# A two-layer hybrid attention trunk: all projections by rows, transposes for q, k and gates on VectorE and DMA, rotation by rows

## The chip, the cores and the metric

The kernel runs on one core of a Trainium2 chip. The metric is the device time of one execution in microseconds (us). Engines are named as the profile names them: PE is TensorE (PEld its loading of the stationary operand), DVE is VectorE, ACT is ScalarE, POOL is GpSimd, SP is SyncE, which here only issues DMAs.

## The reference

Two layers work on x of 256 rows and 2048 columns, all in float32. Each layer normalises x, multiplies it by one wide matrix, runs four groups of attention (4 heads of 128 each) on the result, gates them, and multiplies their concatenation by a second matrix into the residual sum. Cut to what matters:

```python
h = rms_norm(x, norm_g)
p = split_columns(h @ w_in)                    # w_in: 2048 x 7700
fox  = forgetting_attention(q, k, v, log_sigmoid(p["fox_f"] + fb)) * silu(p["fox_g"])
q1, q2, k1, k2 = rope(diff_q, diff_k)          # partial rotary, 16 of 64 columns
diff = (softmax(q1 k1^T) - lam * softmax(q2 k2^T)) v
diff = rms_norm(diff, diff_norm_g) * (1 - lambda_init) * silu(p["diff_g"])
moba = softmax(rope(mq) rope(mk)^T) mv * silu(p["moba_g"])   # one block of 256 keys: causal attention
gla  = rms_norm(gated_linear_attention(gq, gk, gv, log_a), gla_norm_g) * silu(p["gla_g"])
x = x + concat(fox, diff, moba, gla) @ w_out   # w_out: 2048 x 2048
```

After the second layer x is normalised once more and is the output.

## The kernel before

**Products.** Every float32 operand of a large product is split in two parts, hi and lo (both of the type fp32r, which TensorE multiplies in one pass), and a product is the sum of hi x hi, hi x lo and lo x hi. `hTp` holds both parts of the transposed normalised x, `mTh` and `mTl` those of the transposed attention outputs. The weights stream from DRAM: SP loads a step's block (`raw`, 4 buffers), ScalarE makes its hi half (`hi_of`), VectorE its lo half (`lo_of`), three steps ahead of the product (`parts_of`, `prepare`; 4 buffers for each half).

**Steps.** `_blocks` (L104) lists the blocks of columns of both matrices, `_steps` (L142) cuts each into steps: four K tiles of 128 rows for blocks of up to 264 columns, else two. Both kernels have 304 steps, 152 a layer. In a block of the kind "rows" the activations are stationary and the weights move (up to 512 columns; the result has the rows of x on its partitions). In a block of the kind "cols" the weights are stationary and the activations move, hi and lo side by side, so that the result has the features on its partitions, as q and k are needed in a score. A "cols" block of 512 is made in two halves of 256. In `multiply` (L1272) a step of rows has 12 matmuls of 512 columns, a step of columns 16 of 512 and 256. in layer 0 the steps of the first three blocks (the halves of a column block count as two) take turns by group of four K tiles, since x arrives in four chunks; in layer 1 they stand one block after the other.

**1/rms.** The norm's row factor is applied after the projection. For rows it is a per-partition scale (`rows_of`, L520). For columns `spread_rms` (L491) spreads it over the free axis by two products on TensorE into `rb`, and `summed` and `columns` (L509, L516) add the two halves of a result and multiply by `rb`.

**Order of the work.** `main` (L1364 on) walks over the steps: prepare the weights three steps ahead, multiply, then `tick` the task generators. Each task (an attention group, a chunk of the new x, a gate) goes on to its next `yield` once a step as long as VectorE's and ScalarE's budget of estimated time (`Costed`) allows. A block's result is handled by its function in `dones` once its step is through (`settle`). So a `yield` is the unit of distance between two pieces of work, and all that an engine issues stands in its queue in program order. Tiles between the stages come from pools of fixed size (`Slots`): s4 tiles of 1024 elements (named four, 8 of them), s2 of 512 (two, 6), gates (2), and two PSUM tiles `side` for all products outside the projections.

**Turning.** What must be transposed goes through VectorE and DRAM: `turned` (L296) transposes 32 x 32 blocks with a STREAM_TRANSPOSE; `moved` (L310) writes the tile to DRAM (L316), pauses twice, reads it back with the blocks in their places by four DMAs (L321), and pauses twice more before the reader may be issued. All of these DMAs stand on POOL. The softmax probabilities and the outputs of differential attention and GLA take this way, and so do chunks 0 to 2 of layer 1's x (`make_hT`, L455); chunk 3, the last, is transposed on TensorE (`turn_x`, L293 in the profile). `make_hT`'s squares for the row factor (`square_sum`) run on ScalarE.

**Between the layers.** The last block of layer 0 is w_out's chunk 3; `residual` (L1104) adds each chunk of its result to x on VectorE and starts `make_hT`. Layer 1's first block needs all four chunks of the new `hTp`, chunk 3 last.

**The attention groups.** `softmax` (L735) and `attend_columns` (L793) serve FoX and MoBA: q and k come transposed, the probabilities are turned, the second product has v stationary and the result transposed, as `mT` needs it. Differential attention (`diff`, L994) has the probabilities stationary; they are turned with the order "n" (the head innermost), so that its stationary operand `z1[:, :, 2 * h]` is read with a step of four (z0) or eight (z1) elements. `rotated` (L934) turns q and k by a table of cosines over columns, a shuffle on VectorE and a product on GpSimd (L951). GLA sums q times k over each head's columns by products with the constant `heads` (its diagonal, `dg`) and spreads the result over the identity on GpSimd. Gains of the two inner norms are multiplied on GpSimd, and so are the tables for FoX's forget gates (`fox_forget`).

## Time and profile before

| | |
|---|---|
| device time, median of 3 runs | 953.79 us (953.33 to 955.54) |
| the profiled execution: its time | 948.82 us |
| the profiled execution: span of the trace | 947.0 us |
| busy: TensorE, VectorE, ScalarE, GpSimd | 932.3, 633.5, 474.3, 119.5 us |
| DMA | 186.98 MB in 54693 packets, mean 197 GB/s |

The profile is that of one execution, so its times are compared with its own span. The busy share of an engine tells how much work it has, the chain of work that ended last tells whose work set the end, and the list of waits tells for whom an engine stood. The largest groups after TensorE's products are the weights' halves, here with columns for the line, the engine, the operation, out<-in and count, then busy us, mean ns, and idle time before with its releaser:

```profile
L187 DVE TENSOR_TENSOR lo<-raw,hi 128x1024 fp32r<-128x1024 f32 (+3 forms) x301 | 380.6, 1270 | 264.1 <-ACT hi L187 263.8
L187 ACT ACTIVATE hi<-raw 128x1024 fp32r<-128x1024 f32 (+3 forms) x301 | 317.2, 1059 | 398.3 <-PE mm L289 368.5
```

All VectorE and ScalarE calls that the planner costs are recorded at one line (L187, the wrapper's), so groups are told apart by their tiles.

### The profile page before, as it was taken

The page shows a single profiled execution, that of the slowest core. Times are in us where ns is not written, and L with a number is a line of the kernel's source. Part 1 is how long each engine was busy: PE and PEld are TensorE (multiplying, and loading weights), DVE is VectorE, ACT ScalarE, POOL GpSimd, SP SyncE. Part 2 cuts the span into 40 slices and gives each one's busy share as a digit, 9 for nine tenths or more (in the row PEclk, how much of TensorE's full clock was granted, in tenths as well). Part 3 has the DMA queues.
Part 4 walks back from the last instruction along what each step waited for, and adds up shares of the span by engine and source line. Part 5 has one row for each costly group of instructions (what it writes and reads, how often), then busy time and mean ns, then how long its engine had stood idle before and what let it go on. Part 6 is the DMA issues. An engine that isn't in the chain of part 4 may idle for free.

```text
span 947.0 us, 13818 instructions
## 1 busy us (share of the span) xinstructions
PE 932.3 (98%) x5334; PEld 817.7 (86%) x5334; DVE 633.5 (67%) x852; ACT 474.3 (50%) x644; POOL 119.5 (13%) x140
## 2 busy tenths in 40 slices
PE   9999999999999999999989999999999999999996
PEld 7989889888888988888788898898888898888886
DVE  7666777767668777566556668666675777865563
ACT  7665534554574346455446544455446634554451
POOL 0010201201112211011100102102011031130000
PEclk9999999999999999999989999999999999999999
DMA  8766564875568477677755544657555685677552
GB/s 309 231 204 206 175 199 149 234 220 186 178 191 255 135 224 224 205 223 222 225 158 166 170 154 144 196 186 227 196 178 178 203 235 180 194 239 236 192 178 90
DMA packets 54693, 186.98 MB, mean 197 GB/s; under 512 B 7489, under 2 KB 8033, under 8 KB 54626
## 3 DMA queue, kind: packets, MB, share of 16 engines
q1 hardware_dynamic: 46592, 165.24, 55.0%
q0 software_dynamic: 6256, 18.88, 7.0%
q10 hardware_dynamic: 1778, 1.97, 0.8%
q8 instruction: 42, 0.69, 0.3%
q14 instruction: 25, 0.20, 0.1%
HBM read 175.58 MB, written 10.49 MB: 196 GB/s over the span
## 4 chain that ended last, share of the span: by engine, by line
PE 95%; DMA 2%; DVE 1%; issue 1%; ACT 0%; POOL 0%; POOLq 0%; DVEq 0%; SPq 0%; ACTq 0%
PE mm L289 85%; PE side L289 9%; DVE lo L187 1%; DMA raw<-in_weights 1%; DMA four<-turn 1%; DMA four<-in_xt 0%; DVE xs L187 0%; DVE hTp L187 0%; ACT hTp L187 0%; PE side L293 0%; DVE four L187 0%; POOL four L321 0%; ACT hi L187 0%; POOLq L1407 0%; POOL rf L420 0%
## 5 line engine op out<-in xcount | busy, mean ns | idle before, releaser
L187 DVE TENSOR_TENSOR lo<-raw,hi 128x1024 fp32r<-128x1024 f32 (+3 forms) x301 | 380.6, 1270 | 264.1 <-ACT hi L187 263.8
L187 ACT ACTIVATE hi<-raw 128x1024 fp32r<-128x1024 f32 (+3 forms) x301 | 317.2, 1059 | 398.3 <-PE mm L289 368.5
L289 PE MATMUL mm<-hTp,hi 128*128 128x512 f32 x1120 | 281.9, 394 | 0.0
L289 PEld LDWEIGHTS mm<-hTp,hi 128*128 128x128 f32 x1120 | 201.5, 189 | 37.0 <-issue 0.3
L289 PE MATMUL mm<-hi,hTp 128*128 128x512 f32 (+2 forms) x1024 | 197.5, 340 | 0.0
L289 PEld LDWEIGHTS mm<-hi,hTp 128*128 128x128 f32 x1024 | 161.0, 190 | 21.2 <-issue 0.5
L289 PEld LDWEIGHTS mm<-hTp,lo 128*128 128x128 f32 x1120 | 152.8, 190 | 11.0
L289 PE MATMUL mm<-hTp,lo 128*128 128x256 f32 x1120 | 156.1, 282 | 0.0
L289 PE MATMUL mm<-lo,hTp 128*128 128x512 f32 (+2 forms) x512 | 105.3, 338 | 0.1
L289 PE MATMUL mm<-hi,mTh 128*128 128x512 f32 (+1 forms) x256 | 95.2, 377 | 0.0
L289 PE MATMUL mm<-hi,mTl 128*128 128x512 f32 (+1 forms) x256 | 95.0, 376 | 0.0
L289 PEld LDWEIGHTS mm<-lo,hTp 128*128 128x128 f32 x512 | 81.8, 189 | 10.3 <-DVE lo L187 0.3
L289 PE MATMUL mm<-lo,mTh 128*128 128x512 f32 (+1 forms) x256 | 64.4, 376 | 0.0
L289 PEld LDWEIGHTS mm<-hi,mTl 128*128 128x128 f32 x256 | 48.2, 188 | 9.0 <-DVE mTl L187 0.3
L289 PEld LDWEIGHTS mm<-hi,mTh 128*128 128x128 f32 x256 | 48.2, 188 | 8.6
L289 PEld LDWEIGHTS mm<-lo,mTh 128*128 128x128 f32 x256 | 46.2, 188 | 8.8
L289 PE MATMUL side<-four,four 128*128 128x128 f32 (+1 forms) x320 | 41.0, 289 | 0.0
L289 PEld LDWEIGHTS side<-four,four 128*128 128x128 f32 (+1 forms) x320 | 38.0, 205 | 1.9 <-issue 1.4
L951 POOL TENSOR_TENSOR four<-four,two 128x1024 f32<-128x1024 f32 x8 | 20.9, 2607 | 109.4 <-DVE four L187 54.1
L321 POOL DMA_DIRECT2D four<-turn x52 | 28.4, 553 | 34.6 <-DMA turn<-four 16.8
L187 ACT ACT_TABLE_LOAD x24 | 30.8, 1283 | 1.9 <-DVE an L187 1.5
L187 DVE TENSOR_TENSOR both<-mm,both 128x512 f32<-128x512 f32 x35 | 23.9, 682 | 0.0
(160 smaller groups left out, 635.3 us busy)
## 6 DMA issues: line engine op xcount, KB each, us to landing
raw<-in_weights SPq DMA_DIRECT2D x272, 512.0 KB, 4.0
raw<-in_weights SPq DMA_DIRECT2D x16, 516.0 KB, 3.6
raw<-in_weights SPq DMA_DIRECT2D x15, 528.0 KB, 4.6
turn<-four POOLq DMA_DIRECT2D x13, 512.0 KB, 3.4
four<-turn POOLq DMA_DIRECT2D x52, 128.0 KB, 5.8
xs<-in_x SPq DMA_DIRECT2D x4, 512.0 KB, 4.6
four<-in_xt SPq DMA_DIRECT2D x3, 512.0 KB, 6.7
turn<-two POOLq DMA_DIRECT2D x6, 256.0 KB, 4.1
```

Source lines behind the costliest of these rows:

```text
L187: return f(*args, **kw)
L289: t_.matmul(out, lhsT, rhs, start=start, stop=stop)
L321: g_.dma_start(t[c * 32:(c + 1) * 32].rearrange("p q a b -> p q (a b)"), z[:, c].rearrange("(q i) e -> i q e", q=4))
L951: g_.tensor_mul(sw, sw, over(f[:, 1], H))
```

## The change

- **Form.** All blocks are rows now; nine blocks of 512 per layer (GLA's q and k in one, FoX's, differential attention's and MoBA's q and k, FoX's and MoBA's gates) change from columns. `spread_rms`, `summed`, `columns`, `gate_columns` and the tables over columns go.
- **Turning.** `projected` scales such a block on ScalarE (the gates with the SiLU in the same instruction), rotates it by rows where asked (`rotated`, on VectorE, with tables for each row), and turns it with `turned`, so each goes through DRAM. q of all groups and GLA's q and k are then copied by ScalarE into a tile whose columns are in their natural order (`natural_of`); k stays in the order of the turning, and the scores read it as `kT[:, :, kt * H + h]`.
- **Pauses.** `moved` has a third pause between the reads and the reader.
- **Differential attention** turns its probabilities in the order "j" and copies them with `natural_of` before the second product. The outputs of differential attention and GLA are copied the same way, and the norms' gains become this copy's per-partition scale.
- **GpSimd's products.** The tables of FoX's gates and GLA's diagonal are made on ScalarE, head by head; GLA's diagonal sums are made on VectorE from the rows.
- **Order of blocks.** Differential attention's q and k come ahead of FoX's second v block, and its gate behind MoBA's k. In layer 1 the first and third block take turns; the third accumulates in a `side` tile, in layer 0 as well.
- **x.** Chunks 0 and 1 of layer 1's x: ScalarE copies the product to `xs`, and a DMA on POOL adds the input x to it in place (`accum_op`); SP no longer loads these chunks of x. s4 has 10 tiles in place of 8.

```diff
@@ _blocks, _steps
+        for i, (c0, n) in enumerate((
+            (COL["gla_a"], 264),
+            (COL["gla_q"], 512),
+            (COL["gla_g"] + 248, 264),
...
+            (COL["fox_q"], 512),
+            (COL["fox_k"], 512),
+            (COL["diff_q"], 512),
+            (COL["diff_k"], 512),
+            (COL["fox_v"], 258),
+            (COL["fox_g"], 512),
+            (COL["diff_v"], 512),
+            (COL["moba_q"], 512),
+            (COL["moba_k"], 512),
+            (COL["diff_g"], 512),
+            (COL["moba_g"], 512),
+            (COL["moba_v"], 512),
+        )):
+            out.append(block("w_in", l, c0, n, "rows", turn=l if i in ((0, 1, 2), (0, 2))[l] else None))
...
-            key = (j // 4, i) if i < 3 else (9, i)
+            key = (i, 0, 0) if turn is None else (first.setdefault(turn, i), j // 4, i)
@@ moved, behind the four reads
         yield
         yield
+        yield
@@ make_hT
+        if l == 1 and chunk < 2:
+            c = slice(chunk * 512, chunk * 512 + 512)
+            yield
+            g_.dma_start(xs[:, :, c], x[0, :, c].rearrange("(m p) c -> p m c", p=P), accum_op=OP.add)
+            for _ in range(4):
+                yield
@@ row_stats: spread_rms, over, summed, columns go
-        yield from spread_rms(l, r)
...
-        v_.tensor_mul(store[:, half * 2:half * 2 + 2], summed(ps), over(env["rb", l], 2))
...
+    def natural_of(t, slots, parts=((slice(None), 1.0),)):
+        z = yield from slots.take([P, t.shape[2], P])
+        for part, scale in parts:
+            a_.activation(z[:, part].rearrange("p n (q j) -> p n q j", q=4), t[:, :, part].rearrange("p q n j -> p n q j"),
+                          AF.Copy, scale=scale)
+        slots.put(t)
+        return z
+
+    def projected(name, pool=None, heads_first=False, func=AF.Copy, turn=None, natural=None):
+        def done(l, ps):
+            nat = s4.get([P, 8, P])
+            rows_of(l, ps, nat.rearrange("p (a m) d -> p m a d" if heads_first else "p (m a) d -> p m a d", m=2), func)
+            tasks.append(run(l, nat))
+            return nat
+
+        def run(l, nat):
+            yield
+            if turn is not None:
+                yield from rotated(nat, *turn)
+            t, = yield from turned([(nat, pool or s4, "j")], lambda: s4.put(nat))
+            if natural:
+                t = yield from natural_of(t, s4, natural)
+                yield
+            env[name, l] = t
+            ready.add((name, l))
+
+        return done
+
+    def rotated(nat, name, half, width):
...
+        v_.tensor_mul(u, z[..., :rot], cos)
+        v_.tensor_mul(w[..., :half], z[..., half:rot], sin[..., :half])
+        v_.tensor_mul(w[..., half:], z[..., :half], sin[..., half:])
+        v_.tensor_add(z[..., :rot], u, w)
+        s2.put(t)
@@ finish_rows
-        yield from split_group(l, gi, t, lambda: s4.put(t), lambda z: z.rearrange("p h (m q j) -> p q (h m) j", m=2, q=4))
+        z = yield from natural_of(t, s4, ((slice(None), gain[:, 0 if gi == 1 else 1, l:l + 1]),))
+        yield
+        yield from split_group(l, gi, z.rearrange("p (h m) t -> p h (m t)", m=2), lambda: s4.put(z))
@@ gla_qk, gla
+        v_.scalar_tensor_tensor(own, nat[:, 0:4], 0.125, nat[:, 4:8], op0=OP.mult, op1=OP.mult)
+        dgs = sm.tile([P, 8], F32, name="dgs", bufs=2)
+        v_.tensor_reduce(dgs, own.rearrange("p n (x d) -> p n x d", x=2), axis=AX.X, op=OP.add)
...
-                matmul(dg[:, c:c + 2], own[:, pair, m * P:(m + 1) * P], heads, True, True)
...
-        g_.tensor_mul(sT.rearrange("p m h t -> p (m h) t"), ident[:, None, :].to_broadcast([P, 8, P]),
-                      dgs[:, :, None].to_broadcast([P, 8, P]))
+        for m in range(2):
+            for h in range(H):
+                c = (h // 2 * 2 + m) * 2 + h % 2
+                a_.activation(sT[:, m, h], ident, AF.Copy, scale=env["gla_dgs", l][:, c:c + 1])
+            yield
@@ softmax
-                    matmul(dst[:, h], qT[:, h, m * P:(m + 1) * P], kT[:, h, kt * P:(kt + 1) * P],
+                    matmul(dst[:, h], qT[:, m * H + h], kT[:, :, kt * H + h],
@@ fox_forget
-                g_.tensor_mul(z[:, m], after[:, None, :].to_broadcast([P, H, P]), pf[:, m, :, None].to_broadcast([P, H, P]))
+                for h in range(H):
+                    a_.activation(z[:, m, h], after, AF.Copy, scale=pf[:, m, h:h + 1])
+                yield
@@ diff
-        t0, t1 = yield from turned_p(p0[:, 0], p1[0], "n", s4, p0)
+        t0, t1 = yield from turned_p(p0[:, 0], p1[0], "j", s4, p0)
+        z0 = yield from natural_of(t0, s2)
+        z1 = yield from natural_of(t1, s4)
+        yield
...
-            matmul(o[:, 1, h], z1[:, :, 2 * h], vn[:, 0, h * P:(h + 1) * P], True, False)
+            matmul(o[:, 1, h], z1[:, 2 * h], vn[:, 0, h * P:(h + 1) * P], True, False)
@@ residual
-            for m in range(2):
-                v_.tensor_add(xs[:, m, c], ps[m], xs[:, m, c])
+            if l == 0 and chunk < 2:
+                for m in range(2):
+                    a_.activation(xs[:, m, c], ps[m], AF.Copy)
+            else:
+                for m in range(2):
+                    v_.tensor_add(xs[:, m, c], ps[m], xs[:, m, c])
@@ dones
+            projected("fox_q", natural=whole),
+            projected("fox_k"),
+            projected("diff_q", turn=turn_d, natural=whole),
+            started(diff, projected("diff_k", turn=turn_d)),
+            fox_v,
+            projected("fox_g", sgs, True, AF.Silu),
+            rows_v("diff_v"),
+            projected("moba_q", turn=turn_m, natural=whole),
+            started(moba, projected("moba_k", turn=turn_m)),
+            diff_gate,
+            projected("moba_g", sgs, True, AF.Silu),
+            rows_v("moba_v"),
```

How this moves instructions is seen at three places. The rows below are the engine's instructions in program order: line, operation, out<-in with the elements of the output, and how many alike follow each other.

First TensorE between the layers: the last rows of w_out's chunk 3 (`mm<-lo,mTh`), then layer 1's first block (264 columns, `mm<-hi,hTp`), and among it the eight transposes of chunk 3 of the new x (`side<-ct,xs`). Before:

```order
L289 MATMUL mm<-lo,mTh 128x512 x4
L289 MATMUL mm<-hi,hTp 128x264 x16
L289 MATMUL mm<-lo,hTp 128x264 x8
L293 MATMUL side_4258<-ct,xs 128x128 x8
L289 MATMUL mm<-hi,hTp 128x264 x16
L289 MATMUL mm<-lo,hTp 128x264 x8
L289 MATMUL mm<-hi,hTp 128x264 x16
L289 MATMUL mm<-lo,hTp 128x264 x8
L289 MATMUL mm<-hi,hTp 128x264 x16
L289 MATMUL mm<-lo,hTp 128x264 x8
L289 MATMUL mm<-hTp,hi 128x512 x8
L289 MATMUL mm<-hTp,lo 128x256 x8
```

and now, where `side_4008` is the accumulator of the third block:

```order
L282 MATMUL mm<-lo,mTh 128x512 x4
L282 MATMUL mm<-hi,hTp 128x264 x16
L282 MATMUL mm<-lo,hTp 128x264 x8
L286 MATMUL side_3993<-ct,xs 128x128 x8
L282 MATMUL side_4008<-hi,hTp 128x264 x16
L282 MATMUL side_4008<-lo,hTp 128x264 x8
L282 MATMUL mm<-hi,hTp 128x264 x16
L282 MATMUL mm<-lo,hTp 128x264 x8
```

The first step still stands ahead of the transposes; behind them two steps now follow for each chunk of x, and the 512-column block of GLA's q and k, which came in two halves by columns, comes after both blocks and by rows.

Then ScalarE at the same place: the weights' hi halves (`hi<-raw`), the squares of a chunk (`parts<-xs`), and the hi part of the new x from a turned chunk (`hTp<-four`) or from TensorE's transposes (`hTp<-side`). Before:

```order
L187 ACTIVATE hTp<-four_3928,ngt 128x256 x4
L187 ACTIVATE hi<-raw 128x1024 x4
L187 ACTIVATE two_4117,parts<-xs 128x512
L187 ACTIVATE two_4119,parts<-xs 128x512
L187 ACTIVATE hi<-raw 128x1024 x2
L187 ACTIVATE hi<-raw 128x1056 x2
L187 ACTIVATE hTp<-four_4096,ngt 128x256 x4
L187 ACTIVATE hi<-raw 128x1056 x2
L187 ACTIVATE hi<-raw 128x1024
L187 ACTIVATE hTp<-side_4258,ngt 128x256 x4
```

and now:

```order
L181 ACTIVATE two_3774,parts<-xs 128x512
L181 ACTIVATE two_3776,parts<-xs 128x512
L181 ACTIVATE hi<-raw 128x1024 x3
L181 ACTIVATE two_3844,parts<-xs 128x512
L181 ACTIVATE two_3846,parts<-xs 128x512
L181 ACTIVATE hi<-raw 128x1024 x2
L181 ACTIVATE hTp<-four_3753,ngt 128x256 x4
L181 ACTIVATE hi<-raw 128x1056 x3
L181 ACTIVATE hTp<-four_3823,ngt 128x256 x4
L181 ACTIVATE hi<-raw 128x1056 x2
L181 ACTIVATE hTp<-side_3993,ngt 128x256 x4
```

Chunk 1 is `four_3928` before and `four_3753` now, chunk 2 `four_4096` and `four_3823`. Chunk 1's reader stood ahead of chunk 2's squares and eight halves ahead of chunk 2's reader; now it stands behind these squares and three halves ahead of chunk 2's reader. From the squares of chunk 2 to its reader there were four halves and are five, from that reader to chunk 3's (`hTp<-side`) there were three and are two.

Last GpSimd's queue in layer 0 around MoBA: writes to DRAM (`turn<-`), reads back (`<-turn`), and the products that went. The probabilities of MoBA are `two_3485` and `four_3487`, `four_2828` and `four_3051` the shuffled parts of its q and k, and `four_3128` the output of differential attention. Before:

```order
L951 TENSOR_TENSOR four_2828<-four_2828,two_2740 128x1024
L420 TENSOR_TENSOR rsh<-pw,halfpow 128x8
L316 DMA turn_3152<-four_3128 128x1024
L321 DMA four_3128<-turn_3152 32x4x256 x4
L951 TENSOR_TENSOR four_3051<-four_3051,two_2740 128x1024
L316 DMA turn_3507<-two_3485 128x512
L316 DMA turn_3509<-four_3487 128x1024
L321 DMA two_3485<-turn_3507 32x4x128 x4
L321 DMA four_3487<-turn_3509 32x4x256 x4
```

and now, from MoBA's k (`four_2781`) on, with the output of differential attention in `four_3044`, the gate in `gate_3151` and the probabilities in `two_3194` and `four_3196`:

```order
L309 DMA turn_2801<-four_2781 128x1024
L314 DMA four_2781<-turn_2801 32x4x256 x4
L412 TENSOR_TENSOR rsh<-pw,halfpow 128x8
L309 DMA turn_3069<-four_3044 128x1024
L314 DMA four_3044<-turn_3069 32x4x256 x4
L309 DMA turn_3172<-gate_3151 128x1024
L309 DMA turn_3217<-two_3194 128x512
L309 DMA turn_3219<-four_3196 128x1024
L314 DMA gate_3151<-turn_3172 32x4x256 x4
L314 DMA two_3194<-turn_3217 32x4x128 x4
L314 DMA four_3196<-turn_3219 32x4x256 x4
```

The two rotation products are gone; q (just ahead of these rows) and k go through DRAM, and the gate's write stands ahead of the probabilities' writes and its four reads ahead of their eight.

More of the change, by code (lines that the diff above doesn't have):

```diff
@@ new lines, in rotated @@
+    def rotated(nat, name, half, width):
+        z = nat.rearrange("p (m a) (s w) -> p m (a s) w", m=2, w=width)
+        rot = 2 * half
+        g = z.shape[2]
+        t = yield from s2.take([P, 2, 2, g, rot])
+        u, w = t[:, 0], t[:, 1]
+        cos, sin = (turns[name][:, :, i][:, :, None, :].to_broadcast([P, 2, g, rot]) for i in range(2))
+        v_.tensor_mul(u, z[..., :rot], cos)
[3 more added lines that the diff above has]
+        s2.put(t)
@@ L1172, in hybrid_trunk @@
     for z in _BLOCKS:
-        if z["half"] != 1:
-            l, f = next(dones)
-        own = {COL["diff_q"]: ("rope_d",), COL["moba_q"]: ("rope_m",)}.get(z["c0"] if z["w"] == "w_in" else None, ())
-        blocks.append({"kind": z["kind"], "lhs": hT if z["w"] == "w_in" else mT, "n": z["n"], "per": z["per"],
-                       "done": f and (partial(f, l) if z["half"] is None else partial(f, l, half=z["half"])), "keys": {("r", l), ("rb", l)} | {(k, l) for k in own},
-                       "need": "h" if z["w"] == "w_in" else "m", "l": l})
+        l, f = next(dones)
+        blocks.append({"kind": z["kind"], "lhs": hT if z["w"] == "w_in" else mT, "n": z["n"], "per": z["per"], "done": f and partial(f, l),
+                       "keys": {("r", l)}, "need": "h" if z["w"] == "w_in" else "m", "l": l,
+                       "side": z["turn"] is not None and z["c0"] == COL["gla_g"] + 248})
     plan = []
@@ L1251, in first_rms @@
         power(r, t, 2)
-        yield from spread_rms(0, r)
+        env["r", 0] = r
+        ready.add(("r", 0))
     def parts_of(s):
@@ L1275, in multiply @@
         if s["first"]:
-            b["ps"] = side.get([P, 1024]) if b is blocks[2] else mm.tile([P, 1024], F32, name="mm")
+            while b["side"] and not side.free:
+                tick(False)
+            b["ps"] = side.get([P, 1024]) if b["side"] else mm.tile([P, 1024], F32, name="mm")
         ps = b["ps"]
@@ L1333, in prepare @@
     def prepare(i):
[L1334 to L1335 removed]
+        if 0 < i < 16 and i % 4 == 0:
+            split_xt([i // 4 * 4 + k for k in range(4)])
         if i < len(plan):
```

287 lines of the change are left out of this document (68 added, 219 removed).

## The prediction

> **What bounds the kernel now.** I read the page's busy shares and its chain first, then who waited for whom on TensorE, then the timelines of the stretches that the change touches.
>
> ```profile
> PE 932.3 (98%) x5334; PEld 817.7 (86%) x5334; DVE 633.5 (67%) x852; ACT 474.3 (50%) x644; POOL 119.5 (13%) x140
> PE 95%; DMA 2%; DVE 1%; issue 1%; ACT 0%; POOL 0%; POOLq 0%; DVEq 0%; SPq 0%; ACTq 0%
> PE side L293 <- DVE xs L187: 4.8, 1, 4.8
> PE side L361 <- DVE four L356: 1.3, 1, 1.3
> PE side L289 <- DVE four L187: 0.7, 1, 0.7
> ```
>
> TensorE is busy for 98% and carries 95% of the chain; in the list of waits (the last three rows: us, times, longest) it stops for another engine three times in all. So an edit counts if it shortens TensorE's own stream, removes the 4.8 us wait, or makes a new one. Work moved among VectorE, ScalarE and GpSimd counts only through new waits.
>
> **Projections by rows.** TensorE's timeline, first columns (a step of four K tiles by 256 outputs), then rows (two K tiles by 512 outputs: as many products). Columns: start, length, operation.
>
> ```profile
> 167.26 2.00 PE L289 MATMUL mm<-hTp,hi 128*128 128x512 f32 x8
> 169.10 1.11 PE L289 MATMUL mm<-hTp,lo 128*128 128x256 f32 x8
> 170.05 2.00 PE L289 MATMUL mm<-hTp,hi 128*128 128x512 f32 x8
> ...
> 275.83 1.98 PE L289 MATMUL mm<-hi,hTp 128*128 128x512 f32 x8
> 277.65 1.07 PE L289 MATMUL mm<-lo,hTp 128*128 128x512 f32 x4
> 278.55 1.98 PE L289 MATMUL mm<-hi,hTp 128*128 128x512 f32 x8
> ```
>
> From start to start a columns step takes 170.05 - 167.26 = 2.79 us with 16 matmuls, a rows step 2.72 us with 12. Nine blocks of 512 per layer change form: 9 x 8 x 2 = 144 steps, 144 x 0.07 = **-10.1 us**. Per matmul, 512 columns take 1.82 / 8 = 0.228 us and 256 take 0.95 / 8 = 0.119, which is 5 ns over half; over nothing but the 576 dropped matmuls the saving would be worth 17 ns each. The Trainium skill ("TensorE: Matmul & The Clock Gate", section "Back-to-back issue gap") gives a gap of N/2.4 + 2.5 ns: by it the 576 matmuls save 1.4 us, an estimate from that page. The measured steps above differ from it, and I go by them; that it is right after all is a rival below.
>
> **Differential attention's second product.** It now reads copies made contiguous by ScalarE, where before its stationary operand was read with a step of four or eight elements. Before, and beside it the same number of matmuls in MoBA, whose moving operand comes in runs of 32:
>
> ```profile
> 306.39 2.02 PE L289 MATMUL side<-four,two 128*128 128x128 f32 x8
> 308.24 3.97 PE L289 MATMUL side<-four,four 128*128 128x128 f32 x16
> 311.97 2.07 PE L289 MATMUL mm<-hTp,hi 128*128 128x512 f32 x8
> ...
> 386.57 0.38 PE L289 MATMUL side<-two,four 128*128 128x128 f32 x2
> 388.80 0.61 PE L289 MATMUL side<-four,four 128*128 128x128 f32 x4
> 389.17 0.48 PE L289 MATMUL mm<-hi,mTh 128*128 128x512 f32 x1
> ```
>
> 24 matmuls take 311.97 - 306.39 = 5.58 us, MoBA's 24 take 389.17 - 386.57 = 2.60. The new stationary operand is contiguous as MoBA's is: 2 x 2.98 = **-6.0 us**. The scores of all three attentions now stream k in runs of 32, which by the MoBA rows costs nothing.
>
> **Side products dropped.** The spreading of 1/rms over columns and GLA's diagonal sums leave TensorE:
>
> ```profile
> 494.47 0.60 PE L289 MATMUL side<-ct,rstd 128*128 128x128 f32 x4
> 494.83 1.40 PE L289 MATMUL mm<-hTp,hi 128*128 128x512 f32 x5
> ...
> 68.84 0.95 PE L289 MATMUL side<-ct,two 128*128 128x2 f32 x8
> 69.64 1.19 PE L289 MATMUL mm<-hi,hTp 128*128 128x512 f32 x4
> ```
>
> 0.36 + 0.80 us a layer, **-2.3 us**.
>
> **The boundary of the layers.** The 4.8 us wait, by engine (in brackets: idle before, and what ended it), and two windows (length, PE busy, granted clock, DMA share and GB/s):
>
> ```profile
> 449.93 1.28 DVE L187 TENSOR_TENSOR xs<-mm,xs 128x512 f32<-128x512 f32 x2
> 452.26 2.15 DVE L187 STREAM_TRANSPOSE four<-xs 128x512 f32<-128x512 f32 x2
> 454.71 0.56 POOL L316 DMA_DIRECT2D turn<-four  x1 [16.80 <-DVE four L187]
> 461.90 2.19 POOL L321 DMA_DIRECT2D four<-turn  x4 [6.63 <-issue]
> 469.12 2.87 ACT L187 ACTIVATE hTp<-four,ngt 128x256 fp32r<-128x256 f32 x4 [5.97 <-DMA four<-turn]
> 473.00 2.43 DVE L187 TENSOR_TENSOR lo<-raw,hi 128x1056 fp32r<-128x1056 f32 x2 [0.30 <-ACT hi L187]
> 475.35 1.28 DVE L187 TENSOR_TENSOR xs<-mm,xs 128x512 f32<-128x512 f32 x2
> 470.16 1.13 PE L289 MATMUL mm<-lo,hTp 128*128 128x264 f32 x8
> 476.09 2.35 PE L293 MATMUL side<-ct,xs 128*128 128x128 f32 x8 [4.80 <-DVE xs L187]
> 470.90:476.10 5.20, 0.40 (x5) 0.96 0.17 36
> 476.10:483.20 7.10, 6.98 (x34) 0.55 0.62 195
> ```
>
> Chunk 2 of the new x is turned through DRAM: transposed by 454.4, landed at 469.1. ScalarE stood in its queue for 5.97 us; behind it stood the weights' halves, behind those VectorE's sum of chunk 3, and behind that TensorE's transposes. TensorE stood 5.0 us and then ran at a clock of 0.55: the transposes take 478.09 - 476.09 = 2.0 us and the next 16 matmuls 3.66 (481.75 - 478.09, below) where the same 16 before took 1.95 (470.16 - 468.21).
>
> ```profile
> 468.21 2.11 PE L289 MATMUL mm<-hi,hTp 128*128 128x264 f32 x16
> 478.09 3.87 PE L289 MATMUL mm<-hi,hTp 128*128 128x264 f32 x16
> 481.75 0.64 PE L289 MATMUL mm<-lo,hTp 128*128 128x264 f32 x2
> ```
>
> With about 1.1 us too much in the transposes, 1.7 here and 0.4 in the rest of that step, the place costs 5.0 + 3.2 = 8.2 us. The interleaving of layer 1's blocks doubles the work ahead of chunk 3, but the transposes still stand after the first step, so by itself it is worth nothing here. What helps is the third pause in the turning: the reader stands six steps behind, not five (+2.7 us), with one conversion of weights less between it and the sum (-1.2). VectorE is also spared what delayed the sum at 449.93 (chunk 1's reader, which moves behind it), some 1.8 us. Landing at 467.3 plus 5.9 us of that chain is 473.2, against 471.1 for the end of TensorE's step: 2.1 us of standing. Against it, chunk 1's transfers now come just ahead on GpSimd's queue, for they wait for the new accumulating DMA of x; I add 1.1 us. TensorE stands 3.2 us at its own clock: **-5.0 us**. Bounds: landing as before leaves 3.9 us and the slow clock (-1.1); landing ahead of the reader leaves 0.6 (-7.6).
>
> **New transfers and who waits.** Nine more tiles a layer go through DRAM: 18 x 5 = 90 more DMAs on GpSimd, and 18 x 1.05 MB = 19 MB more.
>
> ```profile
> DMA packets 54693, 186.98 MB, mean 197 GB/s; under 512 B 7489, under 2 KB 8033, under 8 KB 54626
> 433.00:438.00 5.00, 5.00 (x24) 4.14 (x23) 2.45 (x2) 1.73 (x3) 2.19 (x4) 1.00 1.00 315
> L321 POOL DMA_DIRECT2D four<-turn x52 | 28.4, 553 | 34.6 <-DMA turn<-four 16.8 <-issue 16.8 <-DMA two<-in_const 1.1
> four<-turn POOLq DMA_DIRECT2D x52, 128.0 KB, 5.8
> 378.14 2.18 POOL L321 DMA_DIRECT2D four<-turn  x4 [0.24 <-issue]
> ```
>
> The mean rises to about 206 / 0.927 = 222 GB/s, under the 315 that a full window moved. An issue costs GpSimd 0.55 us (90 x 0.55 = 50 us, for the 50 us of products that leave it). A DMA on GpSimd is issued behind those before it, and each of the readers stands three pauses after its issue; ScalarE's copies that wait there have the hi halves of later weights behind them. Those run three steps ahead (8.2 us), less 2.3 for the two halves: some 6 us of a reader's waiting are free, and the longest wait of a reader above is 5.97, with the reader one step nearer. The Trainium skill ("SBUF — State Buffer", section "Who interferes with whom") says that GpSimd cannot write descriptors while VectorE holds their shared port: it speaks against 90 more such DMAs. In the trace an issue takes 553 ns in the mean with VectorE busy for 67%, so the sum stays; if VectorE's transposes or products held it, each would add its own 1.4 us, still within those 6.
>
> Tightest is MoBA's second product: its last read is issued at 379.8 and lands some 5.8 us later, 385.6, against 386.57 when TensorE takes it: 1.0 us of room. It moves one step earlier (+2.7), but behind four reads of the gate (-2.2) and in a stretch where 3.1 MB of turning meet 4.2 MB of weights in eight steps, 334 GB/s, over the 315. I take 1 us of waiting a layer, **+2.0 us** (bounds 0 and 6).
>
> ScalarE gains some 36 us (copies, per-head products, block evacuations) and VectorE loses about 45 (sums, 1/rms products, shuffles, against nine transposes a layer); at 54% and 62% both are covered by TensorE. The accumulating DMA has no row: between the 3.4 us of a 512 KB write and four times that, 14 us, it ends before its reader, about 15 us later; cost 0. The start and the end (8 us after the last matmul) stay.
>
> **Sum.** -10.1 - 6.0 - 2.3 - 5.0 + 2.0 = -21.4 us on the profiled execution's 948.8 (span 947.0 and 1.8 around it): 927.4. The median of the three runs shown lies 5.0 us higher, at 953.8, and the prediction is for such runs: 953.8 - 21.4 = **932.4 us**.
>
> **Rivals.**
> - *The waits eat a part.* The boundary keeps its stop (-1.1), MoBA waits 3 us a layer (+6): 953.8 - 10.1 - 6.0 - 2.3 - 1.1 + 6 = 940.3. For it: DMA shares of 1.00 around the boundary. Against it: readers a step later.
> - *A matmul costs its columns alone*, so the change of form brings only 1.4 us: 953.8 - (21.4 - 8.7) = 941.1. This is the page's rule above; against it stand 2.79 and 2.72.
> - *Slower: ScalarE's copies wait in its queue.* Seven such copies a layer read turned data. A single turn took 14.7 us at its slowest above and the reader comes some 13.8 us after the transpose; from about 20 us a turn, the weights' halves behind it come late and TensorE stands for the excess. At 23 us, 14 copies x 3 = 42 us: 953.8 - 23.4 + 42 = 972. It decides from 1.7 us a copy (23.4 / 14). For it: transfers overlap in threes (gate, two probabilities). Against it: no such length in this trace, and room in the DMA's mean.
> - *No change* takes the same waits at 1.7 us a copy, 14 x 1.7 = 23.8 against the gains of 23.4: 954.
>
> **Chances.** Forecast 0.74, waits 0.11, columns alone 0.03, slower 0.09, no change 0.03. The forecast's own range is 926 (-26.0, with the boundary at -7.6 and MoBA free, and 2 us for smaller gaps) to 937; up to 943 it takes in the first two rivals. A measurement of this kernel tells 0.2% (1.9 us) from no change. Faster 0.88, same 0.03, slower 0.09.
>
> **What would show it.** TensorE with some 4,730 matmul records instead of 5334 and rows steps of 2.72 us throughout; differential attention's 24 in 2.6 us; no granted clock of 0.55 at the boundary and under 4 us of standing there; MoBA's wait under 2 us. It is wrong if TensorE's list of waits shows hi or lo of weights, or ScalarE's copies waiting over 6 us for a turned tile.

## The result, and the profile after

| | before | changed |
|---|---|---|
| device time, median of 4 runs each | 953.56 us (951.24 to 955.54) | 939.65 us (939.12 to 944.78) |
| ratio to before, 95% interval | | 0.9867 (0.9826 to 0.9908) |
| the profiled execution: time, span | 948.82, 947.0 us | 939.94, 938.1 us |

The change made the kernel faster by 13.9 us by the medians, where 21.4 were forecast. The time lies 7 us above the point and outside the forecast's own range of 926 to 937; it is inside the wider range, up to 943, that takes in the first two rivals. Between the two profiled executions the gain is 8.9 us, because the one of before was faster than all the runs of before that were timed beside it, and that of the changed kernel lies at its median. Medians and ratios here leave out one slow run of one kernel (best2), which took over 1.5% more than that kernel's fastest.

The page of the changed kernel, busy times, DMA and the chain, then TensorE's list of waits (engine, what it waited for: us in all, times, longest):

```profile
PE 917.3 (98%) x4734; PEld 780.8 (83%) x4734; DVE 577.6 (62%) x782; ACT 505.5 (54%) x712; POOL 120.5 (13%) x204
DMA packets 60271, 204.56 MB, mean 218 GB/s; under 512 B 8977, under 2 KB 9265, under 8 KB 60210
PE 88%; DMA 5%; issue 3%; POOL 1%; DVE 1%; ACT 1%; POOLq 0%; DVEq 0%; ACTq 0%
```

```profile
PE side L282 <- DMA four<-turn: 7.8, 2, 4.1
PE side L286 <- DVE an L181: 1.5, 2, 0.8
PE side L286 <- DVE xs L181: 1.4, 2, 1.1
PE side L354 <- DVE four L349: 1.3, 1, 1.3
PE side L282 <- DVE eight L181: 0.3, 1, 0.3
```

600 matmul records fewer are the 576 of the form and the 24 of the dropped side products. TensorE's own stream is shorter, but its share of the chain fell from 95% to 88%: three waits are new or have moved. The 4.8 us for the sum of chunk 3 (`DVE xs`) became 1.4, MoBA's second product now waits twice 4 us for its turned probabilities, and the transposes of `an` in GLA's first block wait twice for VectorE. GpSimd is as busy as before: its products went and 88 DMAs came (90 for the turning and two that add x, less four small loads of constants).

TensorE's timeline of differential attention's second product, after; columns: start, length, operation:

```profile
285.97 1.05 PE L282 MATMUL side<-four,two 128*128 128x128 f32 x8
286.86 1.95 PE L282 MATMUL side<-four,four 128*128 128x128 f32 x16
288.57 1.17 PE L282 MATMUL mm<-hi,hTp 128*128 128x512 f32 x4
```

From 285.97 to 288.57 are 2.60 us, as forecast. At the boundary (the same view; in brackets the idle time before and what ended it) the stop is 1.1 + 0.3 us, with the granted clock at 1.00:

```profile
467.47 1.13 PE L282 MATMUL mm<-lo,hTp 128*128 128x264 f32 x8
469.73 0.33 PE L286 MATMUL side<-ct,xs 128*128 128x128 f32 x1 [1.12 <-DVE xs L181]
470.32 0.98 PE L286 MATMUL side<-ct,xs 128*128 128x128 f32 x7 [0.26 <-DVE xs L181]
471.06 2.18 PE L282 MATMUL side<-hi,hTp 128*128 128x264 f32 x16
```

The 16 matmuls behind the transposes take 2.0 us, not 3.66. What was lost stands at MoBA. GpSimd's queue in layer 0, TensorE beside it, and three windows (length, busy time of PE, PEld, DVE, ACT and POOL, granted clock, DMA share, GB/s):

```profile
359.04 0.56 POOL L309 DMA_DIRECT2D turn<-gate  x1 [11.22 <-DVE gate L181]
362.45 0.56 POOL L309 DMA_DIRECT2D turn<-two  x1 [2.85 <-DVE two L181]
363.57 0.54 POOL L309 DMA_DIRECT2D turn<-four  x1 [0.56 <-DVE four L181]
364.28 2.20 POOL L314 DMA_DIRECT2D gate<-turn  x4 [0.17 <-issue]
366.94 1.63 POOL L314 DMA_DIRECT2D two<-turn  x3 [0.46 <-issue]
369.73 0.55 POOL L314 DMA_DIRECT2D two<-turn  x1 [1.16 <-DMA turn<-four]
371.65 1.21 POOL L314 DMA_DIRECT2D four<-turn  x2 [1.36 <-DMA gate<-turn]
374.40 1.21 POOL L314 DMA_DIRECT2D four<-turn  x2 [1.54 <-DMA gate<-turn]
```

```profile
378.43 0.38 PE L282 MATMUL side<-two,four 128*128 128x128 f32 x2
382.54 1.19 PE L282 MATMUL side<-four,four 128*128 128x128 f32 x4 [3.72 <-DMA four<-turn]
```

```profile
370.20:378.40 8.20, 8.20 (x38) 6.79 (x37) 2.45 (x2) 4.22 (x5) 2.28 (x5) 1.00 1.03 282
378.40:382.60 4.20, 0.48 (x4) 0.28 (x2) 2.12 (x2) 1.17 (x2) 0.00 (x0) 0.96 1.02 297
382.60:386.50 3.90, 3.90 (x23) 3.90 (x23) 0.33 (x1) 0.00 (x0) 0.00 (x0) 0.60 0.76 287
```

The eight reads of the probabilities took from 366.94 to 375.61, 8.7 us. Before they took 4.6 (375.69 to 380.32); the first four of them, in the kernel before:

```profile
375.69 2.21 POOL L321 DMA_DIRECT2D two<-turn  x4 [3.58 <-DMA turn<-two]
```

The last read, issued at 375.06, landed 7.35 us later, at 382.4. TensorE was through with the two matmuls that do not need it at 378.8 and stood until 382.54. Behind the stop it ran at a clock of 0.60. The DMA share is 1.0 in the windows before and during the stop. Layer 1 is the same, with 4.1 us of standing and seven us at a clock of 0.51:

```profile
843.00:850.00 7.00, 6.22 (x26) 5.96 (x27) 2.38 (x2) 1.06 (x1) 0.00 (x0) 0.51 0.99 391
```

In this execution the clock was at half for 3.4 us behind the first stop and for 6.8 us behind the second, so 1.7 and 3.4 us were lost there. With the 7.8 us of standing, the two places cost 12.9 us.

### The profile page after: what moved, and what is told of

It reads as the page before. It is cut to its first block, busy times and chain, and to the rows that moved or that the text cites. A ratio compares the mean times of both kernels' runs of the same rounds, so it can differ in the third digit from the quotient of the medians.

```text
span 938.1 us, 12710 instructions
## 1 busy us (share of the span) xinstructions
PE 917.3 (98%) x4734; PEld 780.8 (83%) x4734; DVE 577.6 (62%) x782; ACT 505.5 (54%) x712; POOL 120.5 (13%) x204
## 4 chain that ended last, share of the span: by engine, by line
PE 88%; DMA 5%; issue 3%; POOL 1%; DVE 1%; ACT 1%; POOLq 0%; DVEq 0%; ACTq 0%
PE mm L282 78%; PE side L282 10%; DMA four<-turn 2%; DMA gate<-turn 2%; DMA turn<-four 1%; POOL four L314 1%; PE side L354 0%; DVE lo L181 0%; ACT hi L181 0%; DVE xs L181 0%; POOL gate L314 0%; ACT L181 0%; DVE four L181 0%; ACT hTp L181 0%; PE side L286 0%
## 5 line engine op out<-in xcount | busy, mean ns | idle before, releaser
L181 ACT ACTIVATE hi<-raw 128x1024 fp32r<-128x1024 f32 (+3 forms) x301 | 317.3, 1059 | 378.8 <-PE mm L282 318.4
L282 PE MATMUL mm<-hi,hTp 128*128 128x512 f32 (+2 forms) x2048 | 465.8, 371 | 0.0
L282 PEld LDWEIGHTS mm<-hi,hTp 128*128 128x128 f32 x2048 | 358.7, 188 | 66.3 <-issue 1.1
L282 PE MATMUL mm<-lo,hTp 128*128 128x512 f32 (+2 forms) x1024 | 249.8, 369 | 0.0
L282 PEld LDWEIGHTS mm<-lo,hTp 128*128 128x128 f32 x1024 | 181.0, 188 | 32.7
L314 POOL DMA_DIRECT2D four<-turn x108 | 59.2, 554 | 76.7 <-DMA turn<-four 38.6
L309 POOL DMA_DIRECT2D turn<-four x27 | 15.4, 569 | 348.0 <-DVE four L181 337.9
L282 PEld LDWEIGHTS side<-four,four 128*128 128x128 f32 (+1 forms) x320 | 37.1, 202 | 10.4 <-issue 9.5
L181 ACT ACTIVATE four<-mm,rstd 128x512 f32<-128x512 f32 (+2 forms) x56 | 33.6, 647 | 3.6 <-DVE fx L181 3.6
L181 DVE STREAM_TRANSPOSE four<-four 128x1024 f32<-128x1024 f32 x24 | 29.6, 1232 | 0.3
L181 ACT ACTIVATE four<-side,nb 128x256 f32<-128x256 f32 (+1 forms) x48 | 20.5, 436 | 2.0 <-DVE nb L181 1.9
L181 DVE COPY_PREDICATED four<-masks,side 128x128 f32<-128x128 uint8 x56 | 19.1, 341 | 1.8
```

The costliest lines, as they stand in the source:

```text
L181: return f(*args, **kw)
L282: t_.matmul(out, lhsT, rhs, start=start, stop=stop)
L309: g_.dma_start(via[-1], t.rearrange("p c a b -> p c (a b)"))
L314: g_.dma_start(t[c * 32:(c + 1) * 32].rearrange("p q a b -> p q (a b)"), z[:, c].rearrange("(q i) e -> i q e", q=4))
```

## The experiments

Each is an edit of the changed kernel, run beside the kernel before on the same chip; times are medians. Not all were run on one chip, so differences between them are also given by their ratios to before. The theory at their start: the forecast's terms hold but for MoBA's wait, which is larger; the rival: the terms themselves (form, boundary) were overrated.

### The form of the projections

```diff
+                if b["cols"]:                       # the nine blocks
+                    for c in range(4):
+                        wc, o = w[:, c * P:(c + 1) * P], ps[:, c % 2 * 512:c % 2 * 512 + 512]
+                        if part == "hi":
+                            matmul(o, wc, hTp[:, kt].rearrange("p z t -> p (z t)"), first and c < 2, False)
+                        else:
+                            matmul(o[:, :SEQ], wc, lh[:, kt], False, last and c > 1)
+                    continue
```

> The changed kernel with the product of the nine blocks a layer in the form by columns again (16 matmuls a step of 512 and 256 columns in place of 12 of 512), written into the same accumulators so that everything behind it runs as in the changed kernel; two of four chunks of outputs fall on each other, so the projections' values are left wrong. The forecast's term: 144 steps of 2.79 in place of 2.72 us, 10.1 us slower, 949 to 950. Theory of cost by columns alone: 1.4 us slower, 941. In the trace the steps of columns should show 2.79 us from start to start.

Measured 949.84 us (ratio to before 0.9962, 0.9944 to 0.9979): 10.2 us above the changed kernel's median, 9.1 by the ratios, whose intervals leave some 4 us on each side. Its TensorE timeline, two steps by columns:

```profile
300.49 2.00 PE L282 MATMUL mm<-hTp,hi 128*128 128x512 f32 x8
302.33 1.12 PE L282 MATMUL mm<-hTp,lo 128*128 128x256 f32 x8
303.29 2.00 PE L282 MATMUL mm<-hTp,hi 128*128 128x512 f32 x8
```

2.80 us from step to step, as before. The form is worth what the steps' difference says, and the cost by columns alone, 1.4 us, is refuted.

### MoBA's wait

Three kernels: the room for GpSimd's descriptors doubled (`dynamic_dma_scratch_size` 4096 to 8192, `T4` 10 to 9), the gate's turn two pauses later, and the gate's turn left out (the gate is then applied in a wrong order). In the second the wait for the gate also moves behind MoBA's second product, which reads only the probabilities and v. Its edit:

```diff
             if turn is not None:
                 yield from rotated(nat, *turn)
+            for _ in range(2 if name == "moba_g" else 0):
+                yield
@@ attend_columns
-        yield from until((name + "_g", l))
+        if name == "fox":
+            yield from until((name + "_g", l))
...
+        yield from until((name + "_g", l))
+        sgT = env[name + "_g", l]
         mixed = yield from s4.take([P, H, SEQ])
```

> The changed kernel with room for twice as many descriptors of GpSimd's DMAs (8192 bytes in place of 4096; one tile less in the pool of 1024-element tiles makes the place, and the order of all instructions stays). In the changed kernel GpSimd stood 1.36 and 1.54 us ahead of the last four reads of MoBA's probabilities in layer 0, put down to the gate's reads. Theory A, the descriptors' room limits how many DMAs GpSimd has under way: these stands go, the last read lands about 3 us earlier, TensorE's wait at MoBA's second product falls from 4 to 1 us a layer and with it the slow clock behind it; 930 to 934 us. Theory B, the transfers themselves are at the limit (windows there show a DMA share of 1.0): the reads are issued earlier and land as late as now; TensorE's wait stays at 3.5 to 4.3 us a layer, the time within 0.2% of the changed kernel's 939.7.

> The changed kernel with MoBA's gate turned two pauses later, so that its write stands behind the writes of MoBA's probabilities and its four reads behind their eight, and with the wait for the gate moved behind MoBA's second product. The bytes are the same. Theory A, the wait at MoBA's second product comes from the gate's DMAs standing ahead of the probabilities' on GpSimd's queue and rings: the wait falls below 1 us a layer, and the time to 927 to 932 us. Theory B, the DMA engines are full with weights and turns, whatever their order: the wait falls by half at most, 935 us or more. A third way: the gate now comes late, and TensorE stands at group 2 of the output projection instead, 938 us or more.

> The changed kernel without the turning of MoBA's gate (VectorE copies the tile where it transposed it, and its one write and four reads through DRAM are left out), so MoBA's gate is applied in a wrong order. Both theories of a cause in the gate's transfers (queue or bandwidth) expect the wait at MoBA's second product to be gone: under 0.5 us a layer, 926 to 931 us. If instead the cause is the transfers of the weights or the probabilities' own turn, the wait stays above 2 us a layer and the time above 934.

Measured: ring 941.84 us (0.9872, 0.9843 to 0.9901), gate_later 930.31 (0.9761, 0.9734 to 0.9787), gate_unturned 929.26 (0.9741, 0.9714 to 0.9769). GpSimd's queue in ring and in gate_later:

```profile
364.00 2.20 POOL L314 DMA_DIRECT2D gate<-turn  x4
366.43 2.17 POOL L314 DMA_DIRECT2D two<-turn  x4 [0.23 <-issue]
370.92 0.55 POOL L314 DMA_DIRECT2D four<-turn  x1 [2.31 <-DMA gate<-turn]
373.26 0.55 POOL L314 DMA_DIRECT2D four<-turn  x1 [1.79 <-DMA gate<-turn]
```

```profile
362.05 0.57 POOL L309 DMA_DIRECT2D turn<-two  x1 [13.77 <-DVE two L181]
362.61 0.56 POOL L309 DMA_DIRECT2D turn<-four  x1
363.71 0.54 POOL L309 DMA_DIRECT2D turn<-gate  x1 [0.54 <-DVE gate L181]
366.73 2.21 POOL L314 DMA_DIRECT2D two<-turn  x4 [2.48 <-DMA turn<-two]
368.93 2.20 POOL L314 DMA_DIRECT2D four<-turn  x4
372.98 1.10 POOL L314 DMA_DIRECT2D gate<-turn  x2 [1.84 <-DMA two<-turn]
```

In ring the stands in GpSimd's queue remain, so their cause is not the room for descriptors, and TensorE waits 7.7 us in all, as in the changed kernel (7.8). The traces show what ends them. GpSimd's DMAs report to eight semaphores in turn (a semaphore is a counter that one instruction raises and another waits for). Each of these stands is a wait for the semaphore of the DMA eight places before. In ring the first read of `four` left at 370.92; eight before it is the gate's first read, which had landed at 370.37. So the stands are waits in the program itself: each of the four reads of `four` has to wait until one of the gate's four reads has landed.

In gate_later the probabilities' eight reads leave in 4.4 us without a stand; the stands now fall on the gate's. Its DMA is just as full, as three windows over the same places show, but TensorE stands 1.0 us (1.3 in layer 1) and keeps its clock:

```profile
370.40:378.60 8.20, 8.20 (x38) 6.79 (x37) 3.68 (x3) 4.27 (x5) 2.92 (x6) 1.00 1.04 261
378.60:382.40 3.80, 2.84 (x26) 2.65 (x24) 1.23 (x1) 1.06 (x1) 0.00 (x0) 1.00 1.02 261
382.40:386.40 4.00, 4.00 (x21) 3.30 (x20) 1.87 (x2) 1.67 (x2) 0.00 (x0) 1.00 0.97 342
```

So both theories held a part. The DMA engines are full in both orders, and the last of the twelve reads landed no earlier in gate_later (384.4) than in the changed kernel (382.4). But the last read of the probabilities landed at 379.9 in place of 382.4, since the gate no longer stood ahead of them in a line that was full. With the gate behind them the same bytes cost 9.3 us less (10.1 by the ratios). Between the two profiled executions it is 10.6 us: the 12.9 of the two stops, less the 2.3 that gate_later still stands. Without the gate's transfers the wait is gone and the time falls by 10.4 us (12.0 by the ratios). The two kernels' intervals overlap, so by these runs most of what the gate's transfers cost comes from their place.

### The boundary of the layers

Four kernels undo the edits there: one block after the other (`turn` for layer 1 empty), the third pause only outside `make_hT`, the sums of chunks 0 and 1 on VectorE, and all three at once.

```diff
-            out.append(block(..., turn=l if i in ((0, 1, 2), (0, 2))[l] else None))
+            out.append(block(..., turn=l if i in ((0, 1, 2), ())[l] else None))   # no_interleave
@@ moved
-        yield
+        if last:                     # pause_x: make_hT passes False
+            yield
@@ make_hT, residual, main          # no_accum
-        if l == 1 and chunk < 2:
+        if False:
-            if l == 0 and chunk < 2:
+            if False:
-        if i in X_AT[2:]:
+        if i in X_AT:
```

> The changed kernel with layer 1's first and third block one after the other again. The forecast gave the interleaving by itself nothing at the boundary: the transposes of chunk 3 stand behind the first step either way, so TensorE's stop there stays at 1.3 + 0.5 us and the time within 1 us of 939.7. Rival, the interleaving is what cures the boundary: chunk 3's halves are then due two steps (5.9 us) earlier, TensorE waits for hTp behind the transposes, 943 or more.

> The changed kernel with two pauses instead of three in the turning of layer 1's x (chunks 0 to 2), all other turning as changed. The forecast's account: the third pause is what cures the boundary. Without it chunk 2's reader stands one step earlier in ScalarE's queue, waits there about 3.5 us instead of 0.8, and the sum and the transposes of chunk 3 come some 2.2 us later: TensorE stops for 3.6 + 0.5 us, with a slow clock behind it up to 3 us more; 942 to 945. Rival, the transfers land early enough by themselves: the stop stays under 2 us, 939 to 941.

> The changed kernel with x's chunks 0 and 1 added on VectorE again (loaded by SP as before, no adding DMA, none of its pauses). The forecast: chunk 1's transfers no longer stand just ahead of chunk 2's (1.1 us better), chunk 1's reader is again ahead of the sum of chunk 2 on VectorE (1.8 us worse); the stop at the boundary grows by about 0.7 us, 940 to 941. Rival: the adding DMA is what makes room on VectorE; the stop grows to 4 us and more, with its slow clock 943 or more.

Measured: no_interleave 938.72 us (0.9853, 0.9811 to 0.9895), pause_x 938.72 (0.9855, 0.9819 to 0.9892), no_accum 942.96 (0.9888, 0.9852 to 0.9923). The third pause, which the forecast had named as the cure, is not needed by itself: in pause_x's profile (of the fastest of its four runs) chunk 2's reader waited 1.2 us and TensorE 0.3. no_accum's profile had the stop again, 4.4 us; its ScalarE timeline shows chunk 2's reader waiting for its turn and the weights' halves right behind it:

```profile
468.37 2.81 ACT L181 ACTIVATE hTp<-four,ngt 128x256 fp32r<-128x256 f32 x4 [4.10 <-DMA four<-turn]
471.08 2.05 ACT L181 ACTIVATE hi<-raw 128x1056 fp32r<-128x1056 f32 x2
```

But the profiled execution was the slowest of its four (945.69), and no_interleave's profile, also the slowest of four (944.35 against 936.47 to 939.13), had a stop of 4.4 us too. A stop that comes and goes between runs of one kernel can't be settled by one profile, so two kernels with MoBA's disturbance removed (on best1, below) were timed in five rounds:

> The kernel best1 with x's chunks 0 and 1 added on VectorE again, as in no_accum, to settle the boundary with less noise from MoBA. Theory from no_accum's trace: without the pauses of the adding DMA, chunk 1's reader stands ahead of chunk 2's sum on VectorE and waits there for its turned tile, so chunk 2's transposes, its turn and its landing come 4 to 5 us later, TensorE stops 4 to 5 us and then runs at a slow clock: 6 to 7 us more than best1, 933 to 935, and in the trace a granted clock of about 0.6 behind the stop. Rival: no_accum's profile was a chance (its runs lie between 940 and 946), and the adding DMA is worth less than 2 us: 928 to 930.

> The kernel best1 with all three edits at the boundary undone: x's chunks 0 and 1 added on VectorE, two pauses in the turning of x, layer 1's first and third block one after the other. ScalarE's order there is then that of the kernel before (four halves, chunk 2's reader, three halves, chunk 3's reader). Undone one at a time none of the three brought the stop back for certain. Theory J, any one of them is enough: with none left, chunk 2's reader waits some 5 us for its turn again, TensorE stops 4 to 5 us and runs slowly behind it, 933 to 935, all runs shifted. Theory L, the stop comes from how long the turn's transfers take in a run, which the work ahead sets (MoBA's late gate and its backlog), not from these edits: the time stays within 2 us of best1's 928.0, with single runs some 6 us above where the stop occurs.

best1_noacc took 926.96 us (0.9733, 0.9707 to 0.9759; all six runs from 926.38 to 929.73): with MoBA's disturbance removed the adding DMA is not needed either, and no_accum's account does not hold there. boundary_old took 935.31 (0.9811, 0.9788 to 0.9834), 7.3 us above best1 (7.0 by the ratios): five of its runs from 933.99 to 936.46, and one at 926.88. The profile was taken of that one; in it chunk 2's reader waited 2.5 us and TensorE 1.3, with the clock kept. So with all three undone the cost is there in five of six runs. With one undone it is not there for certain: two single profiles had the stop, but the medians of no_interleave, pause_x and best1_noacc did not rise, and no_accum's, 3.3 us higher, has an interval that overlaps the changed kernel's. Pairs of edits were not tried. That boundary_old's five runs stood at this place was not seen in a trace; it is argued from the 7.3 us, about one stop with its slow clock (in no_accum's profile 4.4 us of standing and some five us at a clock of 0.51).

### Differential attention's stationary operand

> The kernel best1 with the stationary operand of differential attention's second product read from the same copies with a step of four elements (first half of the rows) and eight (second half), as the kernel before read it; the values are then taken from wrong places and that group's output is not the reference's. The forecast's term: 24 matmuls take 5.58 us in place of 2.60, twice, so 6.0 us slower than best1's 928.0: 934. If the step costs nothing and the kernel before was slow there for another reason (the order in PSUM, the v operand), 928 and 2.6 us in the trace.

```diff
+        y0, y1 = (z.rearrange("p n t -> p (n t)").rearrange("p (t n) -> p t n", t=P) for z in (z0, z1))
-            matmul(o[:, 0, h], z0[:, h], vn[:, 0, h * P:(h + 1) * P], True, True)
+            matmul(o[:, 0, h], y0[:, :, h], vn[:, 0, h * P:(h + 1) * P], True, True)
```

Measured 935.66 us (0.9823, 0.9791 to 0.9855), 7.6 above best1 (8.1 by the ratios). TensorE's timeline:

```profile
285.19 1.91 PE L282 MATMUL side<-four,two 128*128 128x128 f32 x8
286.94 3.97 PE L282 MATMUL side<-four,four 128*128 128x128 f32 x16
290.66 1.62 PE L282 MATMUL mm<-hi,hTp 128*128 128x512 f32 x6
```

5.47 us in place of 2.60 from the same tiles: the step is the cause, 2.9 us a layer. The other 1.9 us are within the spread of the runs and open: the profile, of the slowest of the four (939.79), has 3.4 us of waiting at the boundary, but no faster run was traced.

### What is left, and a faster version

best1 is gate_later with GLA's first block reordered; best2 is best1 with two pauses in place of three in all turning.

```diff
         for m in range(2):
             v_.tensor_scalar(an[:, m], ps[m][:, 0:16], r[:, m:m + 1], None, op0=OP.mult)
+        for m in range(2):
             a_.activation(sg[:, m, :248], ps[m][:, 16:], AF.Silu, scale=r[:, m:m + 1])
```

> The kernel gate_later (MoBA's gate turned behind the probabilities) with one more edit: in GLA's first block both products for the gate's rank (an) stand ahead of both SiLUs. In the changed kernel VectorE's second one waited 1.9 us for ScalarE's first SiLU, and TensorE 0.8 and 0.7 us for it with the transposes of an. If that order is the cause, these waits go: 1.5 to 1.8 us less than gate_later's 930.3, 928.5 to 929. If not, 930.3.

> The kernel best1 with two pauses in place of three in all turning. If the third pause was never needed where it was forecast to be (pause_x had shown it for x), MoBA's probabilities come one or two steps earlier, TensorE's remaining wait at its second product (2.2 us in best1) goes, ScalarE's copies wait 1 to 3 us longer each, which their queue can bear: 925 to 928. If the third pause is what keeps ScalarE's copies from holding up the halves of the weights, TensorE waits for hi or lo in its list of waits, 930 or more.

best1 took 928.02 us (0.9738, 0.9704 to 0.9773). Its median lies 2.3 us below gate_later's, though the intervals overlap; TensorE's wait for `an` has gone from its list:

```profile
PE side L282 <- DMA four<-turn: 2.2, 1, 2.2
PE side L354 <- DVE four L349: 1.3, 1, 1.3
PE side L286 <- DVE xs L181: 0.5, 2, 0.3
PE side L282 <- DVE eight L181: 0.3, 1, 0.3
```

best2 took 938.59 us (0.9856, 0.9812 to 0.9899; five runs from 933.91 to 946.81), 10.6 us more than best1 and 11.2 by the ratios. Its profile is of the slowest of the five:

```profile
PE side L282 <- DMA four<-turn: 10.6, 4, 4.2
PE side L286 <- DVE xs L181: 4.1, 2, 3.8
```

The third pause is worth some 11 us here, though not where it was expected: without it TensorE waits for turned tiles at four places and for the sum at the boundary. (pause_x, which left it out for x alone, lost nothing.) What was expected, hi or lo of weights in its list, is not there. The lowest median is best1_noacc's, 926.96 us, not told apart from best1's: 26.5 less than the 953.45 of before beside it, and 12.7 less than the changed kernel's median.

## Why the prediction came out as it did

- **Form (-10.1)**: right, 9.1 to 10.2 by experiment. The rule of the Trainium skill that it was weighed against ("TensorE: Matmul & The Clock Gate", section "Back-to-back issue gap") gave 1.4; the page gives that formula for a single matmul by itself, and these runs do not agree with 1.4.
- **Differential attention (-6.0)**: right, 2 x 2.87 to 2.98 us by the traces.
- **Side products (-2.3)**: the matmuls are gone from the trace; not tried by themselves.
- **Boundary (-5.0)**: right in direction, too small, and its mechanism as put was wrong in part. By the two profiles it is 6.8 us: before, 4.8 us of standing and 3.4 of slow clock; after, 1.4 us of standing. boundary_old puts the three edits together at 7.0 to 7.3 us, near the forecast's outer bound of 7.6. "What helps is the third pause" did not hold: in pause_x it could be left out, and in best1_noacc the adding DMA; the cost came back with all three undone. The 1.8 us for VectorE's earlier sum of chunk 2 agree with the traces: against TensorE's step at the boundary it stands 1.9 us earlier. Of the interleaving it said "by itself it is worth nothing here"; no_interleave's median of 938.72 agrees, though its one profile had a stop.
- **MoBA's wait (+2.0)**: the step that failed. "I take 1 us of waiting a layer" was the mis-sized term: it cost 9.3 to 12.0 us by experiment and 12.9 in the profiled execution, beyond its upper bound of 6, and the forecast's own sign, "MoBA's wait under 2 us", was missed (7.8 in the list). The place, the cause (behind the gate's reads, in a stretch where the DMA is full) and the direction were right. Two things were missed. The gate was charged with its four issues, 2.2 us, while with eight places on the way it cost the probabilities' reads 4.0 us of issue (8.7 in place of 4.6) and 1.4 us of landing (7.35 in place of 5.98). Before there were 0.8 us of room (the last read landed at 385.75, not at 385.6), and 0.6 more came from the earlier first read. That leaves 4.0 us from the product's start at 378.43 to the last landing at 382.4, which is what the trace shows. And a stop of that length has the slow clock behind it, which was priced at the boundary but not here.
- **A wait that no term held**: the transposes of `an`, 1.5 us in the list of waits; best1, where this wait is gone, lies 2.3 us below gate_later, with overlapping intervals.
- **GpSimd's 90 more DMAs and ScalarE's copies**: covered, as forecast. The adding DMA landed 6.7 and 9.7 us after its two issues, before the transposes that read x, so its cost of 0 held. ScalarE waited for a turned tile once, 0.8 us, at the boundary, and nowhere for those of q, k or the outputs, so the rival "slower" had no ground. Its row in the list of waits:

```profile
ACT hTp L181 <- DMA four<-turn: 0.8, 1, 0.8
```

- **The rivals**: "the waits eat a part" (940.3) came within 1 us of the time, but by another sum: its MoBA term, 6, was well under what was measured, and its standing boundary did not come. Cost by columns alone (941.1) also lies near and is refuted by cols_form. A time near a rival's number is no evidence for it.

With the sizes measured by experiment the sum is -10.1 - 6.0 - 2.3 - 7.3 + 10 + 2.3 = -13.4, against -13.9. Each of these differences of medians is uncertain by 3 to 4 us, and the side products were not measured by themselves, so that the two agree to half a microsecond is luck. By the two profiled executions it is -10.1 - 6.0 - 2.3 - 6.8 + 12.9 + 1.5 = -10.8, against -8.9, which leaves 2 us open. Luck also kept the time inside the wider range: MoBA cost 7 to 11 us more than forecast, and the 2 us more at the boundary took off a part of it. The prediction's "tells 0.2%" was too fine as well: the interval of the ratio is 0.4% on each side.

It also stays open why the profiled execution of before was 5 us faster than the median of its runs. It had the boundary's stop, so the others lost more there or elsewhere, and no trace of them exists.

## What to carry to other kernels

Where transfers that the bound engine waits for share a queue and full DMA engines with transfers that are needed later, their order can be worth nearly as much as leaving the others out (here 9.3 us against 10.4): put the later-needed behind. Price a stop of the matmul engine with the slow clock that follows it, at every place and not only where a trace already shows it. And where a stop comes in some runs only, one profile settles nothing: undo the suspects together as well as one by one, and read the spread of the runs.

## What the runs showed of the hardware that was not expected

- GpSimd had at most eight DMAs under way, in the kernel before and in all later ones. The traces show a wait of the program behind this; a limit of the engine itself was not reached. Its DMAs report to eight semaphores in turn, and wherever one stood "<-DMA gate<-turn" or "<-DMA two<-turn" at MoBA it waited for the one eight places before to land. Twice the room for descriptors did not change it.
- The granted clock fell to half in pieces of 3.4 or 6.8 us, so 1.7 or 3.4 us were lost. Single stops up to 2.2 us (best1, MoBA in layer 1) had none behind them; those from 2.9 us on (best1_strided, MoBA in layer 1) had it, and so had two stops of 0.7 and 2.1 us with two matmuls between them (best2, at 219 to 222 us). The Trainium skill ("TensorE: Matmul & The Clock Gate", section "What's actually happening") names a window of about 3.4 us that runs on by itself, which the lengths of the pieces agree with; why one stop got the long piece and another the short was not tried.
- At MoBA a read of 128 KB landed 6.4 to 9.3 us after its issue with the gate's reads on the way, where it took 5.6 to 6.0 before; the DMA share was about 1.0 in both. Issuing it earlier then lengthened this: the last read of the probabilities in gate_later took 9.3 us, and still landed 2.5 us earlier than in the changed kernel.
